# Hybrid encoder layer on one core: a spectrum product with one sum, and decayed states and a skip term added on TensorE

## Chip, cores and metric

One core of one Trainium2 chip runs the whole layer. The metric is the device time of an execution in microseconds (us). Engines: TensorE (PE; its weight loads are PEld), VectorE (DVE), ScalarE (ACT), GpSimd (POOL), and SyncE (SP), which issues transfers.

## What is computed

One encoder layer on 1024 tokens of width 1024, all in float32. A normalised input is projected, and the columns feed four mixers side by side: a chunkwise retention, a two-sided state-space model (Mamba-2), a long convolution by Fourier transform (Hyena) and a gated delta rule. Their outputs are joined and projected; a mixture of 16 experts and a gated embedding follow. The parts that matter here:

```python
# retention, per chunk c of 128 tokens and per head (4 heads, 64 wide)
u_fwd = einsum('bcjhd,bcjhe->bchde', kc * pw_tail, vc)
def step(S, u): return dec * S + u, S          # dec = gamma_h ** 128
_, prev = lax.scan(step, s0, u_fwd)            # and the same in reverse
o = scores @ vc + (qc * pw_head) @ prev + (qc * pw_tail) @ nxt

# state space
y_f = ssd_chunked(xs, dt_f, ...)               # scores @ xc + decayed states
y = y_f + y_b + xs * d_skip
return rmsnorm(y * silu(z), norm_w)

# Hyena
v_f, f_f = rfft(v, n=2 * L), rfft(filt, n=2 * L)
y = irfft(v_f * f_f, n=2 * L)[:L] + v * bias
```

## The kernel before

The tokens are eight tiles of 128 rows. The program is written as generators that `weave` takes turns from; a scheduler then sets the order of the instructions on each engine. Each engine works through its own list in order, and transfers are issued from the lists of SyncE, ScalarE and GpSimd. At about 545 us the projections are done and one woven stage runs `gdn_out` (the delta rule's gate), the first eight steps of `ret`, `hy` and `ssm` side by side; the rest of `ret` is taken step by step by `out_proj`, which needs a tile of all four mixers.

**`hy`** works in the frequency domain. For each of nine residues `k1`, `forward` transforms the filter (`pf`) and the signal (`pv`) by three matmuls each into PSUM, [128, 2, 256] with real and imaginary halves. ScalarE copies `pf`, scaled, to `F` (L1350). VectorE multiplies `pv` with F's real half (L1355, into `A`) and its imaginary half (L1356, into `B`), and combines the halves crosswise: one difference and one sum of 256 columns (L1357, L1358). `inverse` multiplies `A` back (L1368 to L1370). `idft16` then joins the nine results, its first half on GpSimd, its second on VectorE (L1259, L1260). L1396 gates the output, and `norm_store` (L1081) normalises it on ScalarE and GpSimd and stores it to `MX` from ScalarE's queue through a tile with two buffers.

**`ret`** first runs over the eight tiles forward. GpSimd scales the keys (L1434), four matmuls give the tile's forward and backward contributions `pu` (L1438), ScalarE copies the backward half (L1441), and `decayed` adds the forward half to the decayed state before it, by four VectorE instructions of 64 columns (L1427), into `U`. The backward half is decayed later, by the same four instructions per tile. `attend(t)` then handles tile t from 7 down: transposes of queries and keys (L1454, L1459), scores (L1467), a mask (L1468), eight matmuls that add scores and states (L1471, L1472). `finish` normalises on VectorE (L1478 to L1488).

**`ssm`** runs forward over the tiles for the states, then back from tile 7. `combine` masks the decay matrices `Ed` (L1045, L1046, one of the two products on GpSimd), scales the decayed states (L1054), and multiplies `Ed` with the inputs, eight matmuls into `py` (L1058). Then the output is summed:

```python
nc.gpsimd.tensor_tensor(out=v4(y), in0=v4(xT[:, t]), in1=dsk..., op=OP.mult)      # L1061
for d in range(2):
    (nc.gpsimd, nc.vector)[d].tensor_tensor(out=v4(y), in0=v4(y), in1=y2[:, :, d], op=OP.add)   # L1064
nc.vector.tensor_tensor(out=y, in0=y, in1=py, op=OP.add)                          # L1065
```

**`out_proj`** splits the weights in a coarse half and a remainder (L1620, L1621, L1625), loads a tile of `MX` (L1686), transposes it together with the retention's tile (L1638) and multiplies (L1649 to L1651); routing of the experts follows tile by tile.

## Time and profile before

| | |
|---|---|
| median of 3 runs | 1629.5 us (1626.34 to 1631.87) |
| profiled execution | 1631.96 us, span 1630.1 us |
| TensorE busy | 1494.8 us, 92% |
| VectorE busy | 1200.2 us, 74% |
| ScalarE busy | 860.4 us, 53% |
| GpSimd busy | 558.2 us, 34% |
| mean granted TensorE clock | 0.963 |

The span is cut into stretches by the times at which the stages begin and end. A stretch's row gives the busy time of each engine in it, the granted clock of TensorE and the share of the transfer engines. A row of grouped instructions gives how many there were, their busy time together (overlaps counted once), the mean duration of one in ns, and the idle time of the engine just ahead of them with what ended it. A row of a timeline gives the start, the time that a group of like instructions spans, and in brackets the wait ahead of it. A float32 matmul shows as two instructions in these counts, a transpose as one.

### The profile page before, as it was taken

What the parts mean: (1) busy time and instruction counts of PE and PEld (TensorE: products, weight loads), DVE (VectorE), ACT (ScalarE), POOL (GpSimd) and SP (SyncE); (2) the same over time, 40 slices, a digit from 0 to 9 for tenths busy, and PEclk for the clock granted to TensorE, in tenths of its full rate; (3) what the DMA queues carried; (4) which work ended last, traced back from release to release, by engine and by line L of the source; (5) the groups of instructions that cost most, each with busy time, mean ns of one, the idle gap of its engine ahead of it and who ended that gap; (6) DMA issues with size and microseconds to landing.
All of it is one profiled execution on the core that took longest, in us unless ns stands there. A gap on an engine that the chain in (4) does not pass through costs nothing.

```text
span 1630.1 us, 25864 instructions
## 1 busy us (share of the span) xinstructions
PE 1494.8 (92%) x9084; PEld 1235.3 (76%) x9084; DVE 1200.2 (74%) x2068; ACT 860.4 (53%) x1413; POOL 558.2 (34%) x780
## 2 busy tenths in 40 slices
PE   4999998989999889779997999999898899998997
PEld 4877777988889766668876877886666688887886
DVE  5589876853656578856778898998888887887663
ACT  6255342124553335432324776877776767666662
POOL 3127665675670358462224200101111121121121
PEclk9999999999999899769997999999999999999999
DMA  5213558454654674164346999999999998889771
GB/s 184 61 39 86 158 165 258 118 170 121 181 154 130 223 238 135 58 191 153 133 163 235 365 338 367 322 333 344 347 351 351 347 294 296 312 313 311 237 261 52
DMA packets 200671, 362.53 MB, mean 222 GB/s; under 512 B 62046, under 2 KB 124732, under 8 KB 200285
## 3 DMA queue, kind: packets, MB, share of 16 engines
q1 hardware_dynamic: 169016, 296.13, 52.9%
q0 software_dynamic: 12400, 42.29, 8.6%
q10 hardware_dynamic: 19125, 22.45, 4.1%
q8 instruction: 72, 1.18, 0.3%
q14 instruction: 58, 0.48, 0.1%
HBM read 301.04 MB, written 59.77 MB: 221 GB/s over the span
## 4 chain that ended last, share of the span: by engine, by line
PE 50%; DMA 19%; DVE 16%; issue 7%; ACT 5%; POOL 3%; SPq 0%; POOLq 0%; ACTq 0%; DVEq 0%
PE pj L300 12%; DVE wl L1625 5%; PE pj L318 5%; DMA raw<-in_exp_w_gate_dram 5%; PE ga L1649 5%; PE ga L1651 5%; PE ga L1650 5%; DMA raw<-in_exp_w_up_dram 3%; ACT wh L1623 2%; PE pj L1650 2%; PE pj L1651 2%; PE pj L1649 2%; PE sp L761 2%; DMA a<-H,tidx 1%; DMA raw<-in_exp_w_down_dram 1%
## 5 line engine op out<-in xcount | busy, mean ns | idle before, releaser
L1625 DVE TENSOR_TENSOR wl<-raw,wh 128x1024 fp32r<-128x1024 f32 x340 | 408.9, 1224 | 85.9 <-ACT wh L1623 83.0
L1623 ACT CAST wh<-raw 128x1024 fp32r<-128x1024 f32 x344 | 355.8, 1053 | 138.4 <-DMA raw<-in_exp_w_up_dram 41.5
L1650 PE MATMUL ga<-wl,xh 128*128 128x512 f32 x512 | 206.4, 403 | 5.5 <-DVE wl L1625 5.3
L1651 PE MATMUL ga<-wh,xl 128*128 128x512 f32 x480 | 190.0, 396 | 0.0
L1649 PE MATMUL ga<-wh,xh 128*128 128x512 f32 x480 | 176.9, 407 | 11.9 <-ACT wh L1623 11.7
L318 PE MATMUL pj<-wh,hnh 128*128 128x256 f32 (+1 forms) x384 | 113.7, 297 | 13.4 <-DVE zss L915 8.6
L1650 PEld LDWEIGHTS ga<-wl,xh 128*128 128x128 f32 x512 | 97.8, 191 | 32.9 <-DVE wl L1625 14.3
L2012 POOL DMA_INDIRECT H<-b,pidx x15 | 39.3, 2617 | 238.4 <-ACT b L2011 169.0
L1649 PEld LDWEIGHTS ga<-wh,xh 128*128 128x128 f32 x480 | 90.7, 191 | 35.5 <-ACT wh L1623 17.0
L300 PE MATMUL pj<-hnh,wh 128*128 128x512 f32 x288 | 116.7, 405 | 0.8 <-ACT cin L337 0.8
L300 PE MATMUL pj<-hnh,wl 128*128 128x512 f32 x288 | 115.7, 402 | 0.0
L300 PE MATMUL pj<-hnl,wh 128*128 128x512 f32 x288 | 115.7, 402 | 0.0
L318 PE MATMUL pj<-wh,hnl 128*128 128x256 f32 (+1 forms) x384 | 111.5, 290 | 0.0
L318 PE MATMUL pj<-wl,hnh 128*128 128x256 f32 (+1 forms) x384 | 111.4, 290 | 0.0
L1650 PE MATMUL pj<-wl,hh 128*128 128x512 f32 x256 | 103.9, 406 | 4.5 <-DVE wl L1625 4.5
L1651 PEld LDWEIGHTS ga<-wh,xl 128*128 128x128 f32 x480 | 91.8, 191 | 18.2
L1959 POOL DMA_INDIRECT a<-HN,pidx x16 | 37.6, 2349 | 187.4 <-PE pj L1650 65.5
L1651 PE MATMUL pj<-wh,hl 128*128 128x512 f32 x256 | 100.1, 395 | 0.0
L1649 PE MATMUL pj<-wh,hh 128*128 128x512 f32 x256 | 89.9, 397 | 0.2 <-ACT hh L1639 0.2
L318 PEld LDWEIGHTS pj<-wh,hnh 128*128 128x128 f32 x384 | 75.1, 196 | 15.7 <-issue 8.3
L318 PEld LDWEIGHTS pj<-wl,hnh 128*128 128x128 f32 x384 | 75.3, 196 | 0.6 <-issue 0.5
L318 PEld LDWEIGHTS pj<-wh,hnl 128*128 128x128 f32 x384 | 75.1, 196 | 0.7 <-issue 0.5
(541 smaller groups left out, 3696.1 us busy)
## 6 DMA issues: line engine op xcount, KB each, us to landing
raw<-in_exp_w_down_dram SPq DMA_DIRECT2D x128, 512.0 KB, 5.9
raw<-in_exp_w_gate_dram SPq DMA_DIRECT2D x108, 512.0 KB, 6.9
raw<-in_exp_w_up_dram SPq DMA_DIRECT2D x104, 512.0 KB, 6.1
wraw<-in_w_in_dram SPq DMA_DIRECT2D x30, 512.0 KB, 4.4
g<-WD SPq DMA_DIRECT2D x16, 768.0 KB, 5.4
room<-in_exp_w_up_dram SPq DMA_DIRECT2D x24, 512.0 KB, 4.5
WD<-gB SPq DMA_DIRECT2D x16, 640.0 KB, 3.3
room<-in_exp_w_gate_dram SPq DMA_DIRECT2D x18, 512.0 KB, 6.4
```

The lines of the kernel that those rows point to most:

```text
L300: self.on_pj = nc.tensor.matmul(pj, lhsT=A[:, kt], rhs=B[:, kt, hs], start=i == 0, stop=i == 23)
L318: self.on_pj = nc.tensor.matmul(pj, lhsT=A[:, kt, ts], rhs=B[:, kt, :], start=i == 0, stop=i == 23)
L761: nc.tensor.matmul(po[:, h], lhsT=L[:, h], rhs=S[:, h], start=True, stop=True)
L1623: nc.scalar.copy(h, r)
L1625: e.tensor_tensor(out=l, in0=r, in1=h.bitcast(F32), op=OP.subtract)
L1649: nc.tensor.matmul(ps, lhsT=xh[:, k], rhs=wh[:, hs], start=first, stop=False)
L1650: nc.tensor.matmul(ps, lhsT=xh[:, k], rhs=wl[:, hs], start=False, stop=False)
L1651: return nc.tensor.matmul(ps, lhsT=xl[:, k], rhs=wh[:, hs], start=False, stop=last)
L1959: self.fetched = self.nc.gpsimd.indirect_dma_start(out=xg, out_offset=None, in_=self.HN if src is None else src, in_offset=bass.IndirectOf ...
L2012: nc.gpsimd.indirect_dma_start(out=self.H, out_offset=bass.IndirectOffsetOnAxis(ap=idx[:, :1], axis=0), in_=y, in_offset=None, compute_op= ...
```

## The change

Three edits. In `hy`, ScalarE writes three copies of the filter's spectrum instead of two halves (real, imaginary negated, imaginary), so that the second product can read `pv` with its halves swapped and one add over both halves finishes the complex product. In `ret`, the decay goes to TensorE: four diagonal matrices `dI` (identity times decay, zero for the backward half) are multiplied with the state before and accumulated on the tile's contributions; ScalarE copies the sum to `U`. In `ssm`, GpSimd scales the tile's input by the skip weight in place, TensorE adds it to `py` by four matmuls with the identity, and GpSimd adds the two directions' states.

```diff
--- before.py
+++ after.py
@@ -1053,15 +1053,17 @@
             y2 = T2([128, 4, 2, 64], "sy2", 2)
             nc.vector.tensor_tensor(out=y2, in0=pi.rearrange("p g (e d c) -> p (g e) d c", e=2, d=2),
                                     in1=sc(ex[:, :, 0], t), op=OP.mult)
+
+            nc.gpsimd.tensor_tensor(out=v4(xT[:, t]), in0=v4(xT[:, t]), in1=dsk[:, :, None].to_broadcast([128, 4, 64]),
+                                    op=OP.mult)
             for h in range(4):
+                hs = slice(h * 64, h * 64 + 64)
+                nc.tensor.matmul(py[:, hs], lhsT=self.ident, rhs=xT[:, t, hs], start=True, stop=False)
                 for d in range(2):
-                    nc.tensor.matmul(py[:, h * 64:h * 64 + 64], lhsT=Ed[:, d, h], rhs=xs[:, h, d], start=d == 0,
+                    nc.tensor.matmul(py[:, h * 64:h * 64 + 64], lhsT=Ed[:, d, h], rhs=xs[:, h, d], start=False,
                                      stop=d == 1)
             y = T2([128, 256], "sy", 2)
-            nc.gpsimd.tensor_tensor(out=v4(y), in0=v4(xT[:, t]), in1=dsk[:, :, None].to_broadcast([128, 4, 64]),
-                                    op=OP.mult)
-            for d in range(2):
-                (nc.gpsimd, nc.vector)[d].tensor_tensor(out=v4(y), in0=v4(y), in1=y2[:, :, d], op=OP.add)
+            nc.gpsimd.tensor_tensor(out=v4(y), in0=y2[:, :, 0], in1=y2[:, :, 1], op=OP.add)
             nc.vector.tensor_tensor(out=y, in0=y, in1=py, op=OP.add)
             z = T2([128, 256], "sz", 2)
             nc.sync.dma_start(z, self.ZS[t])
@@ -1346,16 +1348,18 @@
         def forward(k1):
             M = self.dft_mats(k1, 0)
             pf = self.spectrum(zf, k1, M)
-            F = T2([128, 2, 256], "hF", 2)
-            nc.scalar.activation(F, pf, AF.Copy, scale=(1.0 if k1 in (0, 8) else 2.0) / 2048)
+
+            F = T2([128, 3, 256], "hF", 2)
+            n = (1.0 if k1 in (0, 8) else 2.0) / 2048
+            nc.scalar.activation(F[:, ::2], pf, AF.Copy, scale=n)
+            nc.scalar.activation(F[:, 1], pf[:, 1], AF.Copy, scale=-n)
             pv = self.spectrum(z, k1, M)
 
             A = T2([128, 2, 256], "hA", 2)
             B = T2([128, 2, 256], "hB", 1)
             nc.vector.tensor_tensor(out=A, in0=pv, in1=F[:, 0:1].to_broadcast([128, 2, 256]), op=OP.mult)
-            nc.vector.tensor_tensor(out=B, in0=pv, in1=F[:, 1:2].to_broadcast([128, 2, 256]), op=OP.mult)
-            nc.vector.tensor_tensor(out=A[:, 0], in0=A[:, 0], in1=B[:, 1], op=OP.subtract)
-            nc.vector.tensor_tensor(out=A[:, 1], in0=A[:, 1], in1=B[:, 0], op=OP.add)
+            nc.vector.tensor_tensor(out=B, in0=pv[:, ::-1], in1=F[:, 1:3], op=OP.mult)
+            nc.vector.tensor_tensor(out=A, in0=A, in1=B, op=OP.add)
             return A
 
         def inverse(k1, A):
@@ -1427,6 +1431,12 @@
                 nc.vector.scalar_tensor_tensor(U[half[d], t, h], U[half[d], t - 1 + 2 * d, h], decay[h], src[:, h],
                                                op0=OP.mult, op1=OP.add)
 
+
+        dI = T2([128, 4, 128], "rqt", 1)[half[0]]
+        nc.gpsimd.memset(dI[:, :, 64:128], 0.0)
+        for h in range(4):
+            nc.scalar.activation(dI[:, h, 0:64], self.ident[half[0], 0:64], AF.Copy, scale=decay[h])
+
         for t in range(NT):
             kv = T2([128, 4, 256], "rr", 2)
             nc.sync.dma_start(kv[:, 0:2].rearrange("p a b -> p (a b)"), self.RT[t][:, 256:768])
@@ -1436,11 +1446,13 @@
             pu = self.p([128, 4, 64], "sp", 2)
             for h in range(4):
                 nc.tensor.matmul(pu[:, h], lhsT=kk[:, h].rearrange("p a b -> p (a b)"), rhs=v4(kv[:, 1])[:, h],
-                                 start=True, stop=True)
+                                 start=True, stop=t == 0)
+                if t:
+                    nc.tensor.matmul(pu[:, h], lhsT=dI[:, h], rhs=U[half[0], t, h], start=False, stop=True)
             if t:
                 nc.scalar.copy(U[half[1], t - 1], pu[half[1]])
             if t < NT - 1:
-                decayed(0, t + 1, pu[half[0]])
+                nc.scalar.copy(U[half[0], t + 1], pu[half[0]])
             yield
 
         def attend(t):
```

TensorE's list at a step of the retention's forward loop (`pu` is `sp`, the scaled keys `rqh`, the state `rU`, the diagonals `rqt`; `hA` and `raw` belong to the Fourier matmuls). Before:

```order
L1368 MATMUL pj<-hA,hM 128x512
L1369 MATMUL pj<-hA,hM 128x256
L1370 MATMUL pj<-hA,hM 128x256
L1438 MATMUL sp<-rr,rqh 128x64 x4
L1198 MATMUL pj<-raw,hM 128x512
L1199 MATMUL pj<-raw,hM 128x256
```

After (matmuls of the loop are now L1448 and L1451):

```order
L1374 MATMUL pj<-hA,hM 128x256
L1003 MATMUL ga<-sxd,sbT 128x256 x2
L1020 MATMUL tk<-smv,tri 128x512 x2
L1200 MATMUL pj<-raw,hM 128x512
L1201 MATMUL pj<-raw,hM 128x256
L1202 MATMUL pj<-raw,hM 128x256
L1448 MATMUL sp<-rr,rqh 128x64
L1451 MATMUL sp<-rU,rqt 128x64
L1448 MATMUL sp<-rr,rqh 128x64
```

The four matmuls of a step stood together; each head's second matmul now follows its first, and the step is spread between transforms.

ScalarE's list in the same part (`go` is the delta rule's output, stored from this queue; `hF` is F; the state copies are L1441 before, L1453 and L1455 after). Before:

```order
L1374 COPY wh_5852<-pj 128x512
L820 DMA MX<-go 128x256
L1350 ACTIVATE hF<-pj 128x512
L1007 COPY sST<-ga 128x4x64
L996 COPY sbT<-tk 128x256
L997 COPY sxT<-tk 128x256
L820 DMA MX<-go 128x256
L1441 COPY rU<-sp 64x256
L1374 COPY wh_5853<-pj 128x512
```

After:

```order
L1378 COPY wh_5852<-pj 128x512
L820 DMA MX<-go 128x256
L1354 ACTIVATE hF<-pj 128x2x256
L1355 ACTIVATE hF<-pj 128x256
L996 COPY sbT<-tk 128x256
L997 COPY sxT<-tk 128x256
L820 DMA MX<-go 128x256
L1007 COPY sST<-ga 128x4x64
L1453 COPY rU<-sp 64x256
L1455 COPY rU<-sp 64x256
L1378 COPY wh_5853<-pj 128x512
```

The new state copy stands behind the backward copy, and two stores of `go` lie ahead of the pair, between it and the pair before.

TensorE's list at the end of the mixers (`ga<-sxd,sEd` is the state-space product, `rr`, `rqh`, `rqk`, `rS` and `rqt` belong to the attention of `ret`, `tk<-ident` with `rU` and `a` are the projection's transposes). Before, with the eight matmuls of L1471 and L1472 left out that stand behind each L1467:

```order
L1058 MATMUL ga<-sxd,sEd 128x64 x8
L1459 MATMUL sp<-ident,rqh 128x128 x4
L1467 MATMUL sp<-rqk__7151 128x128 x4
...
L1638 MATMUL tk<-ident,rU 128x128 x2
L1454 MATMUL sp<-ident,rr 128x128 x4
L1459 MATMUL sp<-ident,rqh 128x128 x4
L1467 MATMUL sp<-rqk__7222 128x128 x4
...
L1454 MATMUL sp<-ident,rr 128x128 x4
L1638 MATMUL tk<-ident,a_7094 128x128 x2
L1459 MATMUL sp<-ident,rqh 128x128 x4
L1649 MATMUL ga<-wh_7046,xh 128x512
```

After (L1466, L1471, L1479 are the attention's transposes and scores, L1483 and L1484 its last matmuls, L1650 and L1661 the projection):

```order
L1061 MATMUL ga<-sxT,ident 128x64
L1063 MATMUL ga<-sxd,sEd 128x64 x2
L1483 MATMUL sp<-rr,rS 128x64
L1484 MATMUL sp<-rU,rqt 128x64
...
L1466 MATMUL sp<-ident,rr 128x128 x4
L1471 MATMUL sp<-ident,rqh 128x128 x4
L1479 MATMUL sp<-rqk__7188 128x128 x4
L1483 MATMUL sp<-rr,rS 128x64
...
L1650 MATMUL tk<-ident,rU 128x128 x2
L1650 MATMUL tk<-ident,a_7131 128x128 x2
L1661 MATMUL ga<-wh_7083,xh 128x512
```

Behind the last state-space product stood the scores and the end of one tile's attention, all of another and the start of a third; now stand the end of one and all of another.

## Rows read from the trace of the kernel before

**Rows 1.** Page: span, and busy time (share of the span) and instructions of each engine.

```profile
span 1630.1 us, 25864 instructions
...
PE 1494.8 (92%) x9084; PEld 1235.3 (76%) x9084; DVE 1200.2 (74%) x2068; ACT 860.4 (53%) x1413; POOL 558.2 (34%) x780
```

**Rows 2.** Table by stretch: length, busy us of PE, PEld, DVE, ACT, POOL; PEclk; DMA.

```profile
560.00:600.00 40.00, 36.48 (x180) 27.71 (x178) 28.63 (x74) 11.61 (x30) 22.37 (x19) 1.00 0.87 286
600.00:640.00 40.00, 36.56 (x161) 25.34 (x162) 31.62 (x50) 16.91 (x50) 36.34 (x40) 1.00 0.48 155
640.00:684.00 44.00, 34.47 (x182) 26.52 (x182) 42.15 (x104) 23.41 (x57) 20.79 (x25) 0.89 0.23 71
684.00:713.00 29.00, 16.03 (x71) 13.40 (x71) 18.71 (x31) 11.23 (x32) 20.91 (x31) 0.50 0.61 192
713.00:840.00 127.00, 126.13 (x722) 105.87 (x721) 78.85 (x259) 38.06 (x78) 35.27 (x63) 0.98 0.44 152
```

**Rows 3.** Timeline of PE, 590 to 593: start, us, what.

```profile
590.54 1.03 PE L1003 MATMUL ga<-sxd,sbT 128*128 128x256 f32 x4
591.41 1.00 PE L1438 MATMUL sp<-rr,rqh 128*128 128x64 f32 x8
592.25 1.08 PE L1198 MATMUL pj<-raw,hM 128*128 128x512 f32 x2
```

**Rows 4.** Groups by line, DVE, 555 to 700: busy us, mean ns, idle before.

```profile
L1358 DVE TENSOR_TENSOR hA<-hA,hB 128x256 f32<-128x256 f32 x9 | 11.9, 1326 | 0.0
L1046 DVE TENSOR_TENSOR sEd<-sE,sgm 128x512 f32<-128x512 f32 x8 | 8.2, 1019 | 0.9 <-ACT sE L1023 0.9
L1357 DVE TENSOR_TENSOR hA<-hA,hB 128x256 f32<-128x256 f32 x9 | 7.4, 820 | 0.2
...
L1356 DVE TENSOR_TENSOR hB<-pj,hF 128x512 f32<-128x512 f32 x9 | 6.1, 679 | 0.0
...
L1064 DVE TENSOR_TENSOR sy<-sy,sy 128x256 f32<-128x256 f32 x8 | 5.3, 666 | 7.3 <-POOL sy L1064 7.3
...
L1427 DVE SCALAR_TENSOR_TENSOR rU<-rU,sp 64x64 f32<-64x64 f32 x28 | 4.2, 206 | 2.2 <-ACT rU L1441 2.1
```

**Rows 5.** Groups by line, ACT, 555 to 700.

```profile
L1441 ACT COPY rU<-sp 64x256 f32<-64x256 f32 x7 | 2.6, 367 | 11.6 <-PE ga L1032 4.5 <-DVE go L819 3.7 <-PE pj L1370 3.4
...
L1372 ACT COPY wh<-pj 128x256 f32<-128x256 f32 x2 | 0.7, 372 | 1.2 <-PE pj L1366 1.2
```

**Rows 6.** Timeline of PE, 680 to 714.

```profile
680.78 3.31 PE L1058 MATMUL ga<-sxd,sEd 128*128 128x64 f32 x16 [2.14 <-DVE sEd L1046]
...
688.30 0.69 PE L1471 MATMUL sp<-rr,rS 128*128 128x64 f32 x2 [0.68 <-DVE rS L1468]
...
691.77 0.63 PE L1638 MATMUL tk<-ident,rU 128*128 128x128 f32 x2
694.98 1.09 PE L1454 MATMUL sp<-ident,rr 128*128 128x128 f32 x4 [2.58 <-DMA rr<-RT]
...
701.65 1.22 PE L1467 MATMUL sp<-rqk__7222 64*128 64x128 f32 x4 [3.37 <-ACT rqt L1461]
...
712.69 1.09 PE L1459 MATMUL sp<-ident,rqh 128*128 128x128 f32 x4 [4.94 <-DVE rqh L1450]
713.43 0.78 PE L1649 MATMUL ga<-wh,xh 128*128 128x512 f32 x1
```

**Rows 7.** Timeline of DVE, 683 to 712.

```profile
683.00 0.42 DVE L1478 TENSOR_REDUCE rgs<-sp 128x4 f32<-128x256 f32 x1
...
685.88 0.42 DVE L1484 TENSOR_REDUCE rgs<-sp 128x4 f32<-128x256 f32 x1 [0.58 <-ACT sp L1483]
...
702.90 0.42 DVE L1468 TENSOR_TENSOR rS<-sp,rdm 128x256 f32<-128x256 f32 x1 [4.16 <-PE sp L1467]
703.25 8.70 DVE L1621 SCALAR_TENSOR_TENSOR wl<-raw,pcol,wh 128x1024 fp32r<-128x1024 f32 x4
```

**Rows 8.** Waits of ACT, 550 to 890: what for, us in total, times, longest.

```profile
ACT njk L1086 <- DMA MX<-njk: 12.3, 6, 2.8
```

## Prediction

> **What bounds the kernel now.** I read the page first: TensorE is 92% busy over the span [rows 1], so what moves the end is its 135 us of idle time, or work added to it. The table by stretch then shows where the mixers lie [rows 2]. In 560 to 640 TensorE is busy about 36.5 of each 40 us and VectorE 28.6 and 31.6 (stretch A). In 640 to 684 VectorE is busy 42.15 of 44 us (B). In 684 to 713 nobody is full: TensorE has 16.03 of 29 us, at a granted clock of 0.50, the lower of its two levels (1.2 GHz); that is a chain of latencies (C). From 713 the output projection keeps TensorE busy for 126.13 of 127 us (D). What follows starts when D ends.
>
> Is TensorE really full in A? Its timeline shows groups that start right behind each other, four 256-column instructions in 0.87 us, with no wait in any row [rows 3]. The Trainium skill (Perfetto Trace Analysis, Identifying the Most-Contended Engine) calls matmul busy time a bad measure of headroom and weight-load busy time a better one. The trace has 27.71 of 40 us of weight loads in the first half of A [rows 2], so by that rule there would be room, and the sum would be rival 3's. The gapless starts speak against it.
>
> **The spectrum's product.** For each of nine frequencies VectorE loses two adds of 256 columns, 0.82 and 1.33 us in the mean, and gets one of 512 [rows 4]. No row shows that add. It costs no less than 0.68 us, which a 512-column product from PSUM takes, and hardly more than the two together, 2.15 us. I take 1.02 us: the decay mask's product has 512 columns and two SBUF inputs as well [rows 4]. That is 9 x (2.15 - 1.02) = 10.2 us less on VectorE, bounds 0 and 13.2, nearly all in A. ScalarE gets a second scaled copy each time: 0.37 us by its copy of like size [rows 5], 3.3 us in all. It is busy 11.6 and 16.9 of 40 us in A [rows 2], so this hides there, and costs up to its 3.3 us if TensorE waits for that queue.
>
> **The retention's states.** VectorE loses 28 small updates, 4.2 us [rows 4]. ScalarE gets seven copies of 0.37 us [rows 5], and four scalings once before the loop (at most 1.5 us by the same row, while the mixers wait for their first loads; 1.5 us if that cover is gone). TensorE gets 28 matmuls of 64 columns. Four such matmuls (eight instructions) take 0.84 us from start to start [rows 3], so 0.21 each and 5.9 us; bounds 0, if all falls into idle time, and 11.8 at half clock. A wait is added too: a step's second matmul needs the copy made in the step before, and all that is queued behind it on TensorE waits with it (rival 2).
>
> **The direct way.** VectorE loses eight adds, 5.3 us, and with them the 7.3 us that it waited for GpSimd ahead of them [rows 4]. GpSimd has two instructions per tile as before. TensorE gets 32 matmuls: 6.7 us at 0.21, bounds 0 and 13.4.
>
> In all VectorE sheds 10.2 + 4.2 + 5.3 = 19.7 us and TensorE takes on 12.6. What each is worth depends on the stretch, and the order on the engines says how it divides.
>
> **A, to the last inverse matmul.** TensorE's list there has 19 of the 28 new matmuls and 8 of the 32: 27 x 0.21 = 5.7 us. Five state matmuls and two score matmuls have moved behind it, 7 x 0.21 = 1.5 us. VectorE's relief can't shorten a full TensorE, but some of its 3.4 us of idle time in 600 to 640 [rows 2] should go; I take half. 5.7 - 1.5 - 1.7 = **+2.5 us**, bounds 0.8 and 4.2.
>
> **B, to the last product of the state-space mixer.** VectorE's list from its last spectrum add to the last decay mask has 96 instructions before and 90 now. Four of the removed adds and four updates are gone, 4 x 0.67 + 4 x 0.15 = 3.3 us [rows 4]; the rest moved in or out in about equal numbers. TensorE gets 28 more there, 5.9 us on 34.47 busy of 44, which fits; fewer pauses may spare some half-clock time (0.89 granted). I take two thirds of the 3.3: **-2.2 us**, bounds -4 and +3.
>
> **C, the tail.** From the end of the last product, 680.78 + 3.31 = 684.1, to the first projection matmul at 713.43 are 29.3 us [rows 6]. In it TensorE serves two tiles of attention one after the other. The second tile's scores wait 3.37 us for a query copy, and the query transposes of a third wait 4.94 us for VectorE [rows 6], which is in four weight remainders, 8.70 us, behind a mask that waited 4.16 us for TensorE [rows 7]. In the new order 32 matmuls stand here in place of 48: the last eight of tile 7 and all of tile 6. I expect this chain: statistics of tile 7 on VectorE 3.3 us (683.00 to 686.30), the four remainders 8.7, two masks 0.8 [rows 7]; then tile 6's last eight matmuls 3.5 (688.30 to 691.77), four transposes 1.3 [rows 6], and an estimate of 2.3 for five VectorE or ScalarE steps of about 0.45 that release tile 7 and evict the transposes. Together 19.9 us, so **-9.4 us**, bounds -13 and 0.
>
> **D, the projection.** A whole tile of attention has moved from the tail into this full stretch: 8 transposes at 0.14 (four take 1.09 us at half clock [rows 6]) and 12 matmuls at 0.21, **+3.6 us**, bounds 0 and 7. What follows has the same work and starts when D ends.
>
> Sum: 2.5 - 2.2 - 9.4 + 3.6 = **-5.5 us** against the profiled execution's 1631.96 us (its span is 1630.1), so 1626.5 us. That execution lies 2.5 us above the median of the three runs, 1629.5; the forecast of the median is **1624.0 us**, 0.34% less.
>
> **Rivals.**
> 1. *The tail keeps half of its length saved* (no change). ScalarE waited 12.3 us in six pieces for stores to free its output buffer [rows 8], with query copies and the projection's evictions behind them in its queue, and none of these stores is removed. If they take half of the tail's gain, the sum is -5.5 + 4.7 = -0.8: 1628.7 us. For it: every engine is partly idle in C. Against: a tile of attention is gone from there.
> 2. *TensorE waits for the state copies* (slower). ScalarE's queue stood idle 11.6 us before these copies, waiting for other things, 4.5 us at the longest [rows 5]. That cost TensorE little. Now the decay matmul in full stretch A needs the copy, and in the new order up to two stores of the delta-rule output, each waiting for VectorE, stand ahead of one copy. With all 11.6 us handed on the sum is +6.1: 1635.6 us. It decides once a copy comes later than the 10 to 21 matmuls that lie between two steps, some 3 us. Against: before, such waits fell on steps that the scheduler had no reason to hurry.
> 3. *TensorE has room in A* (faster). The new matmuls vanish between others, and A gains the 3.4 us of idle time where I have +2.5: -5.5 - 5.9 = -11.4, 1618.1 us.
>
> **How the numbers follow.** No change means within 0.3%, 4.9 us, about what a measurement of this kernel can tell. The forecast (0.38) and rival 3 (0.07) make faster 0.45, rival 1 makes same 0.35, rival 2 slower 0.20. The range reaches from 4 us below rival 3, since the tail's bound lies 3.6 us below what I took, to rival 2: 1614 to 1636. The forecast's own range is 1619 to 1627.
>
> **What would show it.** The spectrum's add near 1.0 us; VectorE some 15 us less busy in A; the last inverse matmul 2 to 3 us later in A than before; some 20 us from the last state-space product to the first projection matmul. It is wrong if TensorE shows waits for the state copies in A, if the tail stays near 29 us, or if D grows by more than one tile of attention.

## The result, and the profile after

The changed kernel is slower: 1644.76 us median of 10 runs against 1636.23 us for the kernel before in 10 runs beside it. The ratio is 1.0057, 95% interval 1.0033 to 1.0082, or 5.4 to 13.4 us lost. The forecast was 1624.0 us in a range of 1614 to 1636, and a ratio of 0.9966. The kernel before is itself 6.7 us above the median of the three runs that the forecast started from, so the ratio is the fairer measure; by it the sign was wrong too.

The page of the changed kernel, answering to [rows 1]:

```profile
span 1639.0 us, 26105 instructions
...
PE 1521.2 (93%) x9204; PEld 1262.0 (77%) x9204; DVE 1184.7 (72%) x2023; ACT 868.0 (53%) x1433; POOL 544.9 (33%) x781
```

Its table by stretch, with the columns of [rows 2]:

```profile
560.00:600.00 40.00, 40.00 (x181) 29.01 (x180) 24.19 (x49) 13.57 (x37) 20.65 (x21) 1.00 0.80 261
600.00:640.00 40.00, 40.00 (x199) 29.92 (x198) 24.20 (x39) 21.92 (x59) 36.42 (x41) 1.00 0.48 148
640.00:684.00 44.00, 41.57 (x197) 33.25 (x196) 36.12 (x78) 21.97 (x57) 22.27 (x32) 0.76 0.25 74
684.00:713.00 29.00, 22.04 (x88) 19.28 (x88) 17.39 (x39) 10.02 (x28) 20.33 (x32) 0.50 0.57 195
713.00:840.00 127.00, 126.60 (x735) 106.44 (x734) 78.40 (x254) 36.13 (x72) 30.25 (x51) 0.98 0.42 147
```

VectorE got the relief that was meant: 48.4 us busy in 560 to 640, where it had 60.3. But TensorE now has no idle time there, and from 640 to 684 it is busier (41.57 us against 34.47) at a lower granted clock (0.76 against 0.89). Its timeline there shows two things (start, us, what, wait ahead of it):

```profile
636.59 0.39 PE L1061 MATMUL ga<-sxT,ident 128*128 128x64 f32 x2
636.81 0.61 PE L1063 MATMUL ga<-sxd,sEd 128*128 128x64 f32 x4
637.26 0.39 PE L1061 MATMUL ga<-sxT,ident 128*128 128x64 f32 x2
...
647.67 0.33 PE L1448 MATMUL sp<-rr,rqh 128*128 128x64 f32 x2
647.93 0.43 PE L1451 MATMUL sp<-rU,rqt 64*128 64x64 f32 x2
648.29 0.43 PE L1448 MATMUL sp<-rr,rqh 128*128 128x64 f32 x2
648.66 0.43 PE L1451 MATMUL sp<-rU,rqt 64*128 64x64 f32 x2
...
650.29 0.33 PE L1061 MATMUL ga<-sxT,ident 128*128 128x64 f32 x2
651.51 1.43 PE L1035 MATMUL ga<-sST,sxb 128*128 128x256 f32 x4 [0.88 <-DVE sy L1054]
652.74 0.95 PE L1063 MATMUL ga<-sxd,sEd 128*128 128x64 f32 x4
653.48 0.64 PE L1061 MATMUL ga<-sxT,ident 128*128 128x64 f32 x2
653.90 1.06 PE L1063 MATMUL ga<-sxd,sEd 128*128 128x64 f32 x4
654.76 0.64 PE L1061 MATMUL ga<-sxT,ident 128*128 128x64 f32 x2
...
670.18 3.13 PE L1020 MATMUL tk<-smv,tri 128*128 128x512 f32 x4
673.14 0.33 PE L1061 MATMUL ga<-sxT,ident 128*128 128x64 f32 x2
```

First, the retention's product (L1448) and its new decay matmul (L1451) come in turns, and from start to start each takes 0.36 us, at a granted clock of 1.00; the product alone took 0.21 at the same clock [rows 3]. Second, the direct way's new matmul with the two products behind it (L1061, L1063) took 0.67 us at 636.59, three matmuls of 0.22, and takes 1.28 us at 653.48, after a pause of 0.88 us: the granted clock is 0.50 by then. It stays there until some 672.

To compare kernels I cut the mixers and the projection at the same events in each: **A** from the first state-space state matmul to the end of the last inverse transform, **B** to the end of the last state-space product, **C** to the first projection matmul, **D** to the last router matmul. Of each I take from the table by stretch, in slices of half a microsecond, three sums: TensorE's busy time times the granted clock (its *work*, as it would take at full clock), the rest of the busy time (*low*, what the lower clock costs), and the idle time. Both kernels were profiled twice (the second profiles are e8 and e13):

| us | A | B | C | D | sum | work | low | idle |
|---|---|---|---|---|---|---|---|---|
| before | 83.3 | 45.9 | 29.3 | 144.0 | 302.4 | 249.8 | 20.1 | 32.5 |
| before again (e8) | 82.0 | 46.2 | 27.7 | 142.0 | 297.9 | 249.6 | 20.2 | 28.1 |
| after | 84.7 | 53.4 | 19.2 | 152.9 | 310.2 | 269.6 | 28.5 | 12.1 |
| after again (e13) | 86.1 | 47.1 | 27.8 | 150.1 | 311.1 | 271.1 | 18.2 | 21.8 |
| after less before, means | +2.8 | +4.2 | -5.0 | +8.5 | +10.5 | +20.7 | +3.2 | -13.4 |

What follows D takes 777.3 us (after) against 776.3 (before) in the means, and what precedes A 1.0 us more, so most of the loss lies in these four stretches: 20.7 us more work, of which the idle time swallowed 13.4. The work is the firm number here: 249.8 and 249.6 in the two executions of before. The sum is not; it differs by 4.6 us between those two, and what follows D by 7.

### The profile page after: what moved, and what is told of

It reads as the page before. It is cut to its first block, busy times and chain, and to the rows that moved or that the text cites. A ratio compares the mean times of both kernels' runs of the same rounds, so it can differ in the third digit from the quotient of the medians.

```text
span 1639.0 us, 26105 instructions
## 1 busy us (share of the span) xinstructions
PE 1521.2 (93%) x9204; PEld 1262.0 (77%) x9204; DVE 1184.7 (72%) x2023; ACT 868.0 (53%) x1433; POOL 544.9 (33%) x781
## 4 chain that ended last, share of the span: by engine, by line
PE 63%; DMA 15%; DVE 11%; ACT 4%; issue 4%; POOL 2%; SPq 0%; POOLq 0%; ACTq 0%; DVEq 0%
PE pj L300 12%; PE ga L1661 6%; PE ga L1663 6%; PE ga L1662 6%; DMA raw<-in_exp_w_gate_dram 5%; DVE wl L1637 4%; PE pj L318 4%; DMA raw<-in_exp_w_up_dram 3%; PE pj L1662 3%; PE pj L1661 3%; PE pj L1663 3%; ACT wh L1635 2%; PE sp L761 2%; PE sp L1650 1%; PE ga L1063 1%
## 5 line engine op out<-in xcount | busy, mean ns | idle before, releaser
L1661 PE MATMUL ga<-wh,xh 128*128 128x512 f32 x480 | 177.5, 408 | 10.7 <-ACT wh L1635 9.9
L1661 PEld LDWEIGHTS ga<-wh,xh 128*128 128x128 f32 x480 | 91.3, 192 | 34.0 <-ACT wh L1635 14.5
L1663 PEld LDWEIGHTS ga<-wh,xl 128*128 128x128 f32 x480 | 92.2, 192 | 18.6
L1971 POOL DMA_INDIRECT a<-HN,pidx x16 | 26.3, 1644 | 198.2 <-PE pj L1662 68.7
L1661 PE MATMUL pj<-wh,hh 128*128 128x512 f32 x256 | 90.0, 398 | 0.2 <-ACT hh L1651 0.2
```

The costliest lines, as they stand in the source:

```text
L1661: nc.tensor.matmul(ps, lhsT=xh[:, k], rhs=wh[:, hs], start=first, stop=False)
L1663: return nc.tensor.matmul(ps, lhsT=xl[:, k], rhs=wh[:, hs], start=False, stop=last)
L1971: self.fetched = self.nc.gpsimd.indirect_dma_start(out=xg, out_offset=None, in_=self.HN if src is None else src, in_offset=bass.IndirectOf ...
```

## Experiments

All ratios are to the kernel before, run on the same chip beside it. The table has the stretches of every kernel that wasn't shown yet, from one profiled execution each, while a ratio comes from all executions. e2's profiled execution was the fastest of its twelve, 8 us below their median.

| | ratio (95%) | A | B | C | D | sum | work | low | idle |
|---|---|---|---|---|---|---|---|---|---|
| e1 spectrum | 0.9961 (0.9940-0.9982) | 79.8 | 45.1 | 28.4 | 144.3 | 297.5 | 249.7 | 19.9 | 27.9 |
| e2 retention | 0.9993 (0.9974-1.0013) | 84.5 | 50.4 | 15.4 | 150.5 | 300.8 | 263.7 | 21.9 | 15.2 |
| e3 direct way | 1.0080 (1.0055-1.0105) | 81.1 | 54.8 | 23.6 | 146.9 | 306.4 | 258.9 | 19.5 | 28.0 |
| e15 the same again | one execution | 79.3 | 54.6 | 24.3 | 146.1 | 304.3 | 258.7 | 18.8 | 26.8 |
| e4 all, direct way wide | 1.0003 (0.9976-1.0031) | 86.0 | 42.8 | 21.8 | 148.6 | 299.3 | 268.2 | 17.7 | 13.4 |
| e14 the same again | one execution | 85.6 | 43.1 | 21.8 | 151.6 | 302.1 | 268.0 | 20.7 | 13.4 |
| e5 spectrum, retention | 1.0011 (0.9988-1.0033) | 84.7 | 48.0 | 15.8 | 151.1 | 299.6 | 262.6 | 22.3 | 14.7 |
| e6 direct way wide | 1.0031 (1.0007-1.0055) | 82.6 | 49.2 | 31.1 | 143.3 | 306.2 | 253.0 | 25.0 | 28.2 |
| e7 spectrum, direct way wide | 1.0003 (0.9982-1.0024) | 80.5 | 49.3 | 29.7 | 142.4 | 302.0 | 253.8 | 22.7 | 25.4 |
| e16 spectrum, direct way | 1.0005 (0.9985-1.0025) | 79.3 | 49.9 | 25.8 | 144.3 | 299.3 | 256.6 | 20.9 | 21.8 |
| e9 retention grouped | 1.0024 (1.0006-1.0041) | 83.6 | 50.4 | 25.0 | 142.2 | 301.3 | 257.2 | 21.2 | 22.8 |
| e10 all, grouped | 1.0021 (1.0000-1.0042) | 83.1 | 51.5 | 14.8 | 153.5 | 302.9 | 268.1 | 16.2 | 18.6 |
| e11 all, wide, grouped | 1.0041 (1.0021-1.0060) | 84.0 | 50.4 | 22.8 | 146.2 | 303.4 | 263.3 | 21.2 | 18.9 |
| e12 spectrum, grouped | 1.0083 (1.0063-1.0103) | 84.8 | 49.7 | 30.4 | 147.5 | 312.4 | 260.6 | 28.0 | 23.8 |
| e17 adds on GpSimd | 1.0021 (0.9993-1.0049) | 81.0 | 45.9 | 32.2 | 142.5 | 301.5 | 248.8 | 27.1 | 25.7 |
| e18 spectrum, adds on GpSimd | 1.0026 (1.0000-1.0051) | 80.9 | 45.7 | 34.5 | 144.4 | 305.5 | 250.1 | 26.6 | 28.8 |

**One edit at a time (e1, e2, e3).** Each has one function's hunk of the change on top of the kernel before; its main lines:

```diff
e1, hy.forward alone:
+            nc.scalar.activation(F[:, 1], pf[:, 1], AF.Copy, scale=-n)
...
+            nc.vector.tensor_tensor(out=B, in0=pv[:, ::-1], in1=F[:, 1:3], op=OP.mult)
+            nc.vector.tensor_tensor(out=A, in0=A, in1=B, op=OP.add)
e2, ret alone:
+                    nc.tensor.matmul(pu[:, h], lhsT=dI[:, h], rhs=U[half[0], t, h], start=False, stop=True)
...
+                nc.scalar.copy(U[half[0], t + 1], pu[half[0]])
e3, ssm.combine alone:
+                nc.tensor.matmul(py[:, hs], lhsT=self.ident, rhs=xT[:, t, hs], start=True, stop=False)
...
+            nc.gpsimd.tensor_tensor(out=v4(y), in0=y2[:, :, 0], in1=y2[:, :, 1], op=OP.add)
```

> Only the spectrum's complex product is changed; no instruction of another part moves. The changed kernel is 0.57% slower than before, and its trace shows 7 us lost between the last inverse matmul and the last state-space product, 10 us in the projection, 6.5 us in the experts. Theory 1 (the direct way's 64-column matmuls fill TensorE behind the inverse transforms, and it then runs them at the lower clock): this edit has no share in the loss. VectorE loses some 10 us in 560 to 640, of TensorE's 3.4 us of idle time there 1 to 3 us go: ratio 0.998 to 1.000. Theory 2 (the second scaled copy on ScalarE is late, and TensorE's next transform waits for it): 9 copies of 0.37 us handed on, ratio 1.001 to 1.002, and rows of TensorE waiting for the spectrum's copy.

> Only the retention's decayed states are on TensorE. Theory 1 (the loss is the direct way's): TensorE gets 28 matmuls of 0.21 us, 5.9 us, of which the full stretch 560 to 640 shows 3 to 4 us, and one tile of attention stands behind the first projection matmul, which lengthens the projection by 4 to 6 us and shortens the tail by 5 to 8 us: ratio 1.000 to 1.003. Theory 3 (the retention's edit makes most of the loss, by the tile that it pushes into the full projection): ratio 1.004 to 1.006, and the state-space stretch as long as before, 46 us from the last inverse matmul to the last state-space product.

> Only the state-space direct way is added by TensorE on the diagonal of ones, in 32 matmuls of 64 columns. Theory 1: most of the loss is here. The stretch from the last inverse matmul to the last state-space product grows from 46 to 51 to 54 us, TensorE is busy in over 90% of it, and its granted clock stays at 0.50 for over 15 us there: ratio 1.003 to 1.006. Theory 3 (the retention's edit makes the loss): VectorE's 5.3 us and its waits are gone and TensorE has room, ratio 0.997 to 1.000.

The spectrum's edit is a gain of 0.39%, 6.4 us, more than was expected of it. The retention's edit is worth nothing either way. The direct way's is the loss: 0.80%, with B 54.8 us long in one profile and 54.6 in the other, and 20.5 us of it at granted clock 0.50 in both. The three ratios alone add up to +0.34%, within the interval of the whole change. Theory 2 (late copies of the spectrum) and theory 3 (the retention) are out; theory 1 (the direct way's narrow matmuls) stands on the part, not yet on its mechanism.

**The direct way in wide matmuls (e4, e6, e7, e16).** One matmul of 256 columns starts a tile's sum in place of four of 64.

e4 has it in the changed kernel, e6 in e3, e7 in e16, which is e3 with the spectrum's hunk:

```diff
+            nc.tensor.matmul(py, lhsT=self.ident, rhs=xT[:, t], start=True, stop=False)
             for h in range(4):
-                nc.tensor.matmul(py[:, hs], lhsT=self.ident, rhs=xT[:, t, hs], start=True, stop=False)
                 for d in range(2):
...
-                                     stop=d == 1)
+                                     stop=h == 3 and d == 1)
```

> The changed kernel with the direct way of a tile added by one matmul of 256 columns in place of four of 64 (eight matmuls in all, not 32). Theory 1: 24 matmuls fewer, 8 x (0.84 - 0.43) = 3.3 us less work on TensorE at full clock, up to twice that at the lower one: 3 to 7 us less than the changed kernel, ratio to before 1.001 to 1.004, and less than 15 us at granted clock 0.50 between the last inverse matmul and the last state-space product. Theory 3: no more than 1 us less than the changed kernel, ratio 1.005 to 1.006.

> Only the direct way is on TensorE, in eight matmuls of 256 columns in place of 32 of 64. Its expert instructions stand in the same order as those of the run with 32. Theory 1 (many narrow matmuls keep TensorE full at the lower clock): the stretch from the last inverse matmul to the last state-space product is 43 to 48 us, against 54.8 with 32, with less than 14 us at granted clock 0.50, against 20.5; ratio to before 1.001 to 1.005, against 1.008. If the width has no effect and the loss is all in the new order: stretch 52 to 56 us and ratio 1.006 to 1.009. Theory 4 as well: experts 762 to 768 us.

> Spectrum changed and the direct way in eight matmuls of 256 columns; the retention is as before. Mixers and projection 5 to 10 us shorter than before's 302.5. With theory 4 (the order of the experts costs some 10 us, it is the third order here too) ratio 0.998 to 1.003; with theory 5, 0.993 to 0.997.

> Spectrum changed and the direct way in 32 matmuls of 64 columns; the pair to the run with eight of 256 (ratio 1.0003; 302.0 us to the last router matmul, TensorE work 253.8). Theory 1: TensorE work 257 to 261 us, ratio 1.003 to 1.008. If the width matters only together with the retention's matmuls: ratio 0.998 to 1.002.

In the whole change the wide form takes back 0.54%, nearly all of the loss, and more than theory 1 gave it. These are rows of stretch B as a whole in the changed kernel, first profile and second:

```profile
634.96:688.34 53.38, 50.95 (x254) 42.15 (x253) 43.13 (x98) 27.95 (x71) 28.63 (x39) 0.76 0.25 77
```

```profile
645.55:692.66 47.11, 43.19 (x254) 35.94 (x253) 42.44 (x93) 27.07 (x68) 27.95 (x36) 0.92 0.29 84
```

And with the wide matmuls, first profile and second:

```profile
637.99:680.81 42.82, 40.32 (x204) 31.45 (x202) 39.82 (x89) 27.12 (x68) 27.09 (x35) 0.86 0.30 87
```

```profile
635.25:678.34 43.09, 40.59 (x204) 31.67 (x202) 39.79 (x89) 27.09 (x68) 27.16 (x35) 0.85 0.29 86
```

The wide kernel has 50 instructions fewer in B and 4 to 5 us less work there (34.5 and 34.4 against 38.2 and 39.4); from A to D it has only 1.4 to 3.1 us less, while the lower clock and the idle time together take 31 and 34 us in place of 41 and 40. The other pairs agree only in part. Alone, the wide form takes 1.0080 to 1.0031, but B is 49.2 us long, not 43 to 48, with 17.1 us at the lower clock, so theory 1's clock half missed. With the spectrum (e7 against e16) the width makes no difference, which is a plain miss. What holds in all surroundings is that the narrow direct way costs: +0.80% on before, +0.44% on the spectrum (e16 less e1), +0.46% on spectrum and retention (the change less e5), each clear of the two intervals taken together. None of these kernels holds TensorE's order fixed, so the matmuls and the order that the scheduler made for them are not told apart.

**Do the edits add up (e5)?** Both `hy`'s and `ret`'s hunks, the direct way as before.

> Spectrum and retention are changed, the direct way is as before. Alone they gave ratios 0.9961 and 0.9993, and their profiles are 4.9 and 1.6 us shorter than before's from the first state-space matmul to the last router matmul. This kernel's list of expert instructions on TensorE has the order of the third and fourth runs, whose experts took 765.5 and 765.8 us from the first group count to the end, against 751.7 (before), 755.8 (spectrum alone), 754.4 (retention alone). Theory 4 (that order itself costs some 10 us): mixers and projection 5 to 8 us shorter than before's 302.5, experts 762 to 768, ratio 0.999 to 1.003. Theory 5 (the experts' time scatters from one execution to the next and has nothing to do with the order): ratio 0.994 to 0.997.

They don't: 1.0011, where 0.9954 was the sum. Stretch A shows where a part of it goes. Its rows as a whole, for before, e1, e2 and e5 in this order:

```profile
554.95:638.21 83.26, 76.21 (x343) 55.17 (x343) 61.30 (x128) 28.60 (x80) 58.06 (x58) 0.98 0.69 227
```

```profile
550.29:630.06 79.77, 76.22 (x343) 55.59 (x344) 55.52 (x120) 32.62 (x93) 59.36 (x57) 0.98 0.74 241
```

```profile
550.71:635.18 84.47, 84.27 (x374) 61.36 (x375) 56.80 (x107) 32.55 (x90) 59.50 (x60) 0.98 0.69 228
```

```profile
552.16:636.89 84.73, 84.53 (x377) 61.71 (x378) 56.40 (x101) 37.10 (x104) 60.30 (x60) 0.98 0.70 228
```

The spectrum shortens A by closing TensorE's gaps (76.2 us busy in 83.3 us, then in 79.8). The retention's matmuls fill those same gaps (84.3 busy in 84.5). With both, A is as long as with the retention alone: what the relief of VectorE frees, the new TensorE work has taken. That is some 3 of e1's 6.4 us; the rest is not placed.

**The price of a decay matmul (e9, e10, e11, e12).** A step's four decay matmuls stand behind its four products, not in turns with them; e10 is the whole change with that, e11 has the wide direct way too, e12 the spectrum and no change to the direct way.

```diff
-                                 start=True, stop=t == 0)
-                if t:
-                    nc.tensor.matmul(pu[:, h], lhsT=dI[:, h], rhs=U[half[0], t, h], start=False, stop=True)
+                                 start=h == 0, stop=t == 0 and h == 3)
+            if t:
+                for h in range(4):
+                    nc.tensor.matmul(pu[:, h], lhsT=dI[:, h], rhs=U[half[0], t, h], start=False, stop=h == 3)
```

> Retention's edit alone, a step's four decay matmuls together behind its four products, in place of in turns. In turns, the retention's edit took 13.9 us more of TensorE's busy time at full clock from the first state-space matmul to the last router matmul (263.7 against 249.8), 0.50 for each of 28 decay matmuls. Theory 6 (a change between weights of 128 and of 64 partitions costs 0.14 to 0.15 us each way; the matmul itself is 0.21): grouped there are 14 changes and not 56, 28 x 0.21 + 14 x 0.15 = 8.0 us, so 257 to 259 us; ratio to before 0.994 to 0.998, against 0.9993 in turns. Theory 7 (a 64-partition matmul is as dear wherever it stands): 262 us or more, ratio 0.998 to 1.001.

> The changed kernel with the decay matmuls grouped, nothing else changed. Theory 6: 5 to 7 us less TensorE work than the changed kernel's 269.5 and so 4 to 9 us shorter: ratio to before 1.000 to 1.003. Theory 7: within 2 us of the changed kernel, 1.005 to 1.007. If most of the loss is the direct way's narrow matmuls (theory 1) the ratio stays over 1.002.

> All three edits, the direct way in eight matmuls of 256 columns and the decay matmuls grouped. Theories 1 and 6 together: TensorE work of before plus 2.8 (direct way wide, measured) plus 8.0, some 260 to 262 us against 269.5, VectorE's relief kept; ratio to before 0.994 to 0.999. Theory 7: as the run with the wide matmuls alone, 0.999 to 1.002.

> Spectrum and grouped retention, direct way as before; the experts stand in the order of the retention run. Theory 6: TensorE work 257 to 259 us, both gains added: ratio 0.991 to 0.996. Theory 7: 0.996 to 1.000. Should the spectrum alone (0.9961) stay the best, then TensorE has no room for either added matmul.

The price that theory 6 puts on a change of weights shows in e9's timeline. The scheduler split the groups there, so that one to four decay matmuls (L1448, two instructions each) stand together; the second row of each pair is what follows:

```profile
584.45 0.43 PE L1448 MATMUL sp<-rU,rqt 64*128 64x64 f32 x2
584.81 1.13 PE L1003 MATMUL ga<-sxd,sbT 128*128 128x256 f32 x4
...
602.01 1.10 PE L1448 MATMUL sp<-rU,rqt 64*128 64x64 f32 x8
603.04 1.12 PE L1198 MATMUL pj<-raw,hM 128*128 128x512 f32 x2
```

From start to start one takes 0.36 us and four take 1.03; two took 0.58 (at 588.15) and three 0.81 (at 575.08), all at a granted clock of 1.00. That is 0.22 for each matmul and 0.14 for the group. In turns every decay matmul is a group of its own, 28 in e2; the grouped kernels have 13 to 16. There the decay matmuls take 8.1 to 8.4 us of work and the products 6.7 to 6.8, where e2 has 10.1 and 8.8. Of TensorE's work as a whole theory 6 is right in e9 alone (257.2 us): e10 has 268.1, e11 263.3 and e12 260.6, all more than it gave. Of e2's 13.9 us more work, 0.50 for each decay matmul as the expectation had it, 2.7 us belong to the attention's scores, which the section on the prediction comes to; in e9 these have gone as well. Of the time theory 6 is wrong in all but e10. The 6.5 us of work that e9 saves against e2 come back as 7.6 us of idle time, and e12 is, with e3, the slowest kernel of all, with 28.0 us lost to the lower clock. The scheduler gave each its own order: e9's C is 25.0 us again, where e2 had 15.4.

**Chance of one execution, and the experts (e8, e13, e14, e15).** Repeats, with no edit: before, after, e4 and e3.

> The kernel before once more, for the scatter of its stretches. Theory 4: experts 750 to 757 us from the first group count to the end, as in the first profile (751.7). Theory 5: anywhere from 750 to 766 us. Mixers and projection within 2 us of 302.5 by either.

> The changed kernel once more. If the long stretch at the lower clock behind the inverse transforms belongs to this order of instructions: 20 to 30 us at granted clock 0.50 between the last inverse matmul and the last state-space product (25.9 in the first profile), TensorE work to the last router matmul 269 to 270 us, time lost to the lower clock there 24 to 30 us, mixers and projection 306 to 312 us. If the first profile's clock was a chance of that execution: under 16 us at 0.50 in that stretch, and 300 to 304 us in all. Experts 754 to 760 us by theory 4; by theory 5 anywhere from 750 to 766.

> All three edits with the direct way in eight matmuls of 256 columns, once more. If the width decides: 8 to 15 us at granted clock 0.50 behind the inverse transforms (11.3 in the first profile), the stretch 41 to 45 us, mixers and projection 297 to 302 us. Experts 762 to 768 by theory 4 (765.8 before), anywhere from 750 to 766 by theory 5.

> The direct way alone in 32 matmuls, once more. Experts 762 to 768 us by theory 4 (765.5 before), anywhere from 750 to 766 by theory 5. Mixers and projection 304 to 308 us, TensorE work there 258 to 260 us.

The long stretch at the lower clock in the changed kernel was a chance of its first execution: in the second B has 7.7 us of it, not 25.9. Yet the sum came out the same, 310.2 and 311.1, and low and idle time together too, 40.6 and 40.0. What the second execution saved in B it lost in C. TensorE's timeline of C in e13:

```profile
695.87 1.06 PE L1466 MATMUL sp<-ident,rr 128*128 128x128 f32 x4
703.57 1.12 PE L1471 MATMUL sp<-ident,rqh 128*128 128x128 f32 x4 [6.63 <-ACT rqk__7188 L1468]
...
713.67 0.69 PE L1483 MATMUL sp<-rr,rS 128*128 128x64 f32 x2 [5.02 <-DVE rS L1480]
...
718.66 0.69 PE L1650 MATMUL tk<-ident,rU 128*128 128x128 f32 x2 [1.31 <-DVE rU L1500]
...
720.45 0.79 PE L1661 MATMUL ga<-wh,xh 128*128 128x512 f32 x1 [0.67 <-ACT xh L1651]
```

and ScalarE's, ahead of the copy that the 6.63 us were spent on:

```profile
702.50 0.42 ACT L1088 ACTIVATE njk<-sy 128x256 f32<-128x256 f32 x1 [4.81 <-DMA MX<-njk]
...
702.93 0.59 ACT L1468 COPY rqk__7188<-sp 128x512 f32<-128x512 f32 x1
```

A copy stands in ScalarE's queue behind an instruction that waits 4.81 us for a store to free its buffer. That is rival 1's mechanism; in the first execution the same copy came 0.68 us late.

Theory 4 (one order of the experts costs some 10 us) falls: kernels with that order, the third, took 765.5, 761.4 (e3, e15), 760.4 (e16), 760.6, 759.7, 758.0 and 757.2 us (e6, e7, e5, e10), and e4 and e14, whose order is all but the same, 765.7 and 759.4; 762 to 768 was expected. The first order took 751.7, 759.0 and 755.8 (before twice, e1), so a difference of a few microseconds is possible and stays open.

**Relief without TensorE (e17, e18).** Both adds of the direct way on GpSimd; TensorE gets nothing. e18 has the spectrum's hunk as well.

```diff
-                (nc.gpsimd, nc.vector)[d].tensor_tensor(out=v4(y), in0=v4(y), in1=y2[:, :, d], op=OP.add)
+                nc.gpsimd.tensor_tensor(out=v4(y), in0=v4(y), in1=y2[:, :, d], op=OP.add)
```

> The kernel before with both adds of the direct way on GpSimd: VectorE is rid of its eight adds, as in the change, and TensorE gets nothing. If VectorE's relief there is worth time and only TensorE's matmuls eat it up: the stretch behind the inverse transforms 1 to 4 us shorter than 45.7 (mean of two profiles of before), ratio 0.997 to 1.000. If the relief is worth nothing because the wait for the product or for GpSimd takes its place: stretch 45 to 48 us, ratio 1.000 to 1.003; the whole of the direct way's loss is then not TensorE's matmuls alone.

> The spectrum's edit and both adds of the direct way on GpSimd. If the relief is worth time: ratio 0.992 to 0.996, below the spectrum's own 0.9961. If not: 0.996 to 1.000, and the spectrum alone stays the best kernel of the study.

B stayed as long as in before: 45.9 us against a mean of 46.0 (not 45.7, as the expectation has it), and C became 3.7 us longer, 32.2 against 28.5. TensorE's waits for VectorE's decay masks in B fell from 5.4 and 4.4 us to 1.9, but those for GpSimd's half of the masks rose from 0.6 to 2.2. In the end nothing was gained (1.0021) and e18 lost what the spectrum had won. So here the relief of VectorE was worth nothing. GpSimd has one add per tile more than in the change, though, so that the relief of the change itself is worth nothing is argued, not shown. **The best kernel of the study is e1**, the spectrum's edit alone, at 0.9961; it is faster than both.

## Why the prediction was wrong

The forecast's sum is 12.6 us more work for TensorE and 18.1 us less of its idle time and lower clock, together -5.5. Measured from A to D were 20.7 more work and 10.2 less of the other two, together +10.5. So about half of the miss is work priced too low, and half is waiting and lower clock that stayed. The work by instruction says which price was wrong (each instruction from its start, or from the end of the one ahead of it, times the granted clock; first profiles):

| us of work, A to D | before | e2 | e3 | after | e9 |
|---|---|---|---|---|---|
| 28 decay matmuls | | 10.1 | | 10.1 | 8.1 |
| 32 products of the retention | 6.6 | 8.8 | 6.8 | 9.1 | 6.8 |
| 32 score matmuls of the attention | 6.8 | 9.5 | 9.4 | 9.4 | 6.5 |
| 32 matmuls of the direct way | | | 6.9 | 6.9 | |
| all others | 236.4 | 235.2 | 235.8 | 234.1 | 235.9 |

The scores' 2.6 us were put at nothing, since no edit touches them. A tile's four score matmuls read two halves of the partitions, two matmuls each, and the scheduler pulled the halves apart. Rows of TensorE at granted clock 1.00, before and then after:

```profile
738.55 0.72 PE L1467 MATMUL sp<-rqk__7515 64*128 64x128 f32 x8
```

```profile
733.62 0.71 PE L1479 MATMUL sp<-rqk__7382 64*128 64x128 f32 x4
...
737.37 0.71 PE L1479 MATMUL sp<-rqk__7382 64*128 64x128 f32 x4
```

Side by side the two halves take 0.72 us together, since their instructions start in pairs, 13 ns apart; apart each half takes 0.71. Five of the eight tiles are split so in the changed kernel, one and a part of another in the kernel before.

- **The spectrum's price: right.** The add was taken at 1.02 us and took 1.005 in the mean. VectorE's group by line in the changed kernel:

```profile
L1362 DVE TENSOR_TENSOR hA<-hA,hB 128x512 f32<-128x512 f32 x9 | 9.0, 1005 | 0.1
```

  Its worth was set too low: 1.7 us in A, where e1 gained 6.4 (2.9 to 9.8).
- **A, +2.5: right in size by luck, wrong in its terms.** A grew by 2.8 us in the means. But its work grew by 8.6 us (74.4 to 82.9), not 4.2, and 6 us of idle time went, not 1.7. "TensorE really full in A" was not so before: 36.48 and 36.56 of 40 us [rows 2] leave 7 us of gaps, of which I had counted only those of the second half. It is full now, 0.2 us idle. The Trainium skill (Perfetto Trace Analysis, Identifying the Most-Contended Engine) holds weight-load time to be the better measure of headroom; with 29.01 of 40 us of weight loads in the table above, that says there is still room. e5 against e1 shows that there is none: A went from 79.8 to 84.7 us when the retention's matmuls came.
- **The retention's term, 5.9 us: a step that failed, by its size.** It is 12.6 us of work: 10.1 for the decay matmuls, 0.36 each, and 2.5 more for the products that stand in turns with them. I took 0.21 from a row where products of one form follow each other [rows 3]. The Trainium skill (TensorEngine Tiling (Array Packing), Key Properties) says that a change of tiling mode drains TensorE. The rows fit that: 0.36 from start to start in turns (647.93, 648.29, 648.66), and in e9 0.14 for a group beyond its matmuls. I had not weighed it. Four of the 28, those of the loop's last step, even make a sum that nothing reads. The price alone is not the loss of time: e2 has it and came to 0.9993.
- **The direct way's term, 6.7 us: right. B, -2.2: a step that failed.** "TensorE gets 28 more there, 5.9 us on 34.47 busy of 44, which fits; fewer pauses may spare some half-clock time (0.89 granted)." The 32 matmuls took 6.9 us of work, 0.22 each. But B grew by 7.3 us in the change's first execution and 1.1 in the second, and by 8.8 and 8.5 in e3 and e15. In e3 and e15 its work grew by 6.7 us in the mean; the idle time, 9.5 and 8.6 us in B before, gave back only 1.8 of them, and the lower clock took 3.6 us more. TensorE's waits in B, in total, times, longest, in the kernel before:

```profile
PE ga L1058 <- DVE sEd L1046: 5.4, 4, 2.1
```

  and in e3:

```profile
PE ga L1063 <- DVE sEd L1046: 4.0, 1, 4.0
PE ga L1032 <- DVE sy L1067: 2.9, 1, 2.9
```

  The waits for VectorE's masks and sums are still there with the new matmuls beside them. I read that as a chain of the two engines, which a longer step of TensorE makes longer; it was not tried apart. In the change, which moves work of the retention here too, the idle time of B did go (2.4 and 3.9 us are left), and 7.3 us of work came. Fewer pauses did not spare the lower clock: e3 had 20.5 us of it in B in both profiles. The two thirds of VectorE's relief that I credited did not show in e17.
- **C, -9.4: -10.2 in the first execution, -1.5 in the second, against the 29.3 that the forecast started from.** The chain went nearly as written, 19.2 us in place of 19.9 from the last product to the first projection matmul in the first profile:

```profile
687.28 1.06 PE L1063 MATMUL ga<-sxd,sEd 128*128 128x64 f32 x4
...
700.76 0.69 PE L1483 MATMUL sp<-rr,rS 128*128 128x64 f32 x2 [3.89 <-DVE rS L1480]
...
705.74 0.69 PE L1650 MATMUL tk<-ident,rU 128*128 128x128 f32 x2 [1.31 <-DVE rU L1500]
...
707.53 0.79 PE L1661 MATMUL ga<-wh,xh 128*128 128x512 f32 x1 [0.67 <-ACT xh L1651]
```

  In the second, ScalarE's wait for a store ate it, as rival 1 had it.
- **D, +3.6: +8.5, above its bound of 7.** Its work grew by 6.6 us (135.7 to 142.3). My 3.6 was one tile's matmuls and transposes. The tile's eight last matmuls came to 1.9 us, but 16 transposes had moved (48 in D against 32), 1.6 us, and the scores took 7.0 us for six tiles where they had taken 3.7 for five. The lower clock took 2.4 us more. So the shorter tail was no gain: e2, where no direct way interferes, has C 13.1 us shorter, and B 4.4 and D 7.5 longer than the means of before.
- **Rival 2** had the right sign for the wrong reason: no wait of TensorE in the changed kernel names the state copies. **Rival 3** is out, as A shows.

What stays open is why the narrow direct way costs time. It adds 6.9 us of work, as forecast, yet one wide matmul in its place, with 1.4 to 3.1 us less work in all, saved 0.54%; the rest is waiting and lower clock in another order, which no run separates. Why C is 15 us long in one order and 34 in another is open too.

## What to carry to other kernels

An engine's idle time in a chain of hand-overs need not be room: before work is moved there, ask whether the idle time lies ahead of that work's consumer, and price the new instruction among the neighbours that it will have, not from a row where its like follow each other. Two edits that use the same gaps don't add up; try each alone first. Where a scheduler sets the order, compare its order before and after, for instructions that no edit touches as well, such as the scores here: the only kernel here that was faster beyond its interval (e1) is also the only one in which TensorE's order stayed as it was, but for two rows.

## What was not expected of the hardware

- Matmuls of 64 columns with weights of 64 and of 128 partitions in turns: 0.36 us each from start to start, against 0.21 for a run of the 128-partition ones; together behind each other, n of the 64-partition ones took 0.14 + 0.22 n us (e9).
- Score matmuls with weights of 64 partitions: those of the lower and the upper half side by side took 0.72 us for both, and 0.71 for each half where other matmuls stood between.
- The changed kernel lost the same 40 us to the lower clock and to idle time in two executions, 28.5 + 12.1 and 18.2 + 21.8, in different places. One profile told the work and the sum of the four stretches, but not the length of a single one (B 53.4 and 47.1, C 19.2 and 27.8).
